# A two-layer diffusion block on one core: fixed gate buffers, a free list of fetch rows, and side work called twice a step

## The chip, the cores and the metric

The kernel runs as one program on one NeuronCore of a Trainium2 chip. The metric is the device time of one execution in microseconds. Three runs of the kernel before took 2971.26, 2975.04 and 2978.68 us; their median, 2975.04 us, is the time before. The core has five instruction streams that run side by side and wait for each other by semaphores: TensorE (PE in the profile; its weight loads are PEld), VectorE (DVE), ScalarE (ACT), GpSimd (POOL) and the stream that issues loads (SP). Each takes its instructions strictly in the order in which they were written.

## The reference

Two layers work on 256 latent tokens and 256 context tokens of width 1024. Each layer mixes tokens (Fourier, pooling and attention branches, gated and projected) and then retrieves experts; the change touches the second half alone:

```python
q = (xc @ wq).reshape(C, PEER_HEADS, 2, PEER_KEY_DIM)
s = jnp.einsum('chpd,hpnd->chpn', q, sub_keys).astype(jnp.float32)
s1, i1 = lax.top_k(s[:, :, 0], PEER_TOPK)
s2, i2 = lax.top_k(s[:, :, 1], PEER_TOPK)
cand = (s1[..., :, None] + s2[..., None, :]).reshape(C, PEER_HEADS, PEER_TOPK * PEER_TOPK)
...
top, pos = lax.top_k(cand, PEER_TOPK)
eidx = jnp.take_along_axis(cidx, pos, axis=-1)
g = jax.nn.softmax(top, axis=-1).astype(xc.dtype)
a = jax.nn.gelu(jnp.einsum('chkd,cd->chk', u_tab[eidx], xc))
return jnp.einsum('chk,chkd->cd', g * a, v_tab[eidx])
```

Each token picks 128 of 16384 experts (8 heads, 16 each). An expert is a row of U and a row of V, 1024 numbers each; a layer's two tables have 64 MB each. The output of layer 1 is that of the latent tokens alone, so layer 0 handles four blocks of 128 tokens and layer 1 two.

## The kernel before, in words

**Dense and fetched blocks.** For all blocks but one the kernel does not gather rows. It multiplies the tokens by the whole table U, applies gelu, multiplies by a gate matrix G (tokens by experts, zero where an expert was not picked) and then by V. In layer 0 three blocks go this way (384 columns) and the fourth is fetched: 128 picks of U rows and 128 of V rows, each a gather of one row per token (`ask`, L945) that VectorE multiplies and sums (`use_one`, L966). In layer 1 both blocks are dense (256 columns) and nothing is fetched.

**The loop over U** (L1114 to L1150) has 64 steps of 256 experts. A step loads 1 MB of U (`raw`, three buffers, L218), transposes it on VectorE (`u_T`, UT, L1011), splits it into a high half on ScalarE (`u_hi`, L1018) and a low half on GpSimd (`u_lo`, L1025), and multiplies: two halves `a` of 24 matmuls each (L282 to L284), each closed by a gelu on ScalarE (L1130). H goes to DRAM (L1132). The transpose runs two steps ahead of the matmuls in layer 0, three in layer 1.

**Side work.** A Python generator, `side`, writes the instructions that pick experts and build G: the top-16 searches on VectorE, then `places` for each block (ending in a reduce of `ii` on VectorE, L854, three transposes on TensorE, L864 to L866, and gL on VectorE, L871), then `gate_matrix`. It yields a cost after each piece. `pump`, called at the end of every step, adds a budget to a debt and goes on writing pieces while the debt is over 2.0; a negative cost means that nothing can be done yet. The budget of a step is 5.4 in layer 0 and 3.2 in layer 1, and 6.6 and 3.8 once the gate matrix has begun. These numbers only set the order in which instructions are written; nothing in the program measures them.

**The gate matrix** takes 8 tokens at a time, a chunk: 48 chunks in layer 0, 32 in layer 1. VectorE writes one-hots by comparing (L890 and L892) and multiplies one of them by the gate (L897; in layer 0 GpSimd does the other half of that multiply, L896; in layer 1 VectorE does it all in L902, and L904 is a part of the low gate); ScalarE scales the one-hots by the low part of the gate (`oh[:, 3]`, L899 or L907). These four one-hots stand in `ohs`, which holds two chunks. TensorE multiplies them, 16 matmuls of 128 columns (L919, L920), and ScalarE moves the two PSUM banks into `stg` (L922). Four chunks fill one `stg`, which ScalarE's queue stores to DRAM as a part of G (L924, 2 MB). In an iteration for chunk c the one-hots of c are written first and the products of c - 1 after them; since `pump` may stop at any yield, the boundary of a call falls in different places. Step 54 writes whatever is left.

**Rows for fetches.** `picked` is two buffers of four rows. Eight rows rotate up to pick 80, four up to pick 128, then eight again, by the fixed table `slot`; a buffer is given back at pick 80 and taken again in the loop over V. In layer 0 112 of the 256 picks are spread over the U loop.

**Buffers.** The pool `b16` has eight buffers of 16 KB a partition for `hl` (split U or V), `hT`, `picked`, `ohs`, `stg`, X and the parts of G and H read back; `b4` has six of 4 KB for gelus, scores and small work. PSUM has six banks for this stage in layer 0, one of them held by `iop`.

**The loop over V** then reads G and H back and multiplies by V, with the same prefetch (`v_load` at step 56 issues the first reads of G on SP's queue).

Of the kernel before, what the change touches and what calls it, by code (L numbers as in the profile page):

```python
# [18 lines left out]
D = 1024  # L19
# [41 lines left out]
def kernel(ctx_: ExitStack, tc: tile.TileContext, I, C, out):  # L61
# [706 lines left out]
    def peer(l, nrm, kT, nb, fin):  # L768
# [52 lines left out]
        def places(b, gT, gL):  # L821
            if True:
# [33 lines left out]
                if b == sparse:  # L856
# [3 lines left out]
                    SP["buf"] = [b16([128, 4, D], name="picked") for _ in range(2)]  # L860
                    SP["ready"] = True
                    return
                ps = psum()
# [10 lines left out]
        def gate_matrix(gT, gL):  # L874
            W = 8
            ohs = b16([128, 2, 4, W, 128], F16, name="ohs")
            hot[0] = True
            iop = psum(name="iop")
            nc.vector.tensor_copy(out=iop[:, :128], in_=iota)
            prev = None  # L880
            stg = None
            for c in range(nt // W + 1):
                cur = None
                if c < nt // W:
                    b, t0 = divmod(c * W, 128)
                    t = gT[b]
                    oh = ohs[:, c % 2]
                    io = iop[:, None, :128].to_broadcast([128, W, 128])
                    bc = lambda q: t[:, q, t0:t0 + W, None].to_broadcast([128, W, 128])
                    nc.vector.tensor_tensor(out=oh[:, 1], in0=io, in1=bc(0), op=OP.is_equal)  # L890
                    yield 1.2
                    nc.vector.tensor_tensor(out=oh[:, 0], in0=io, in1=bc(1), op=OP.is_equal)  # L892
                    if nb == 4:
                        w = W // 2
                        g16 = t[:, 2, t0:t0 + W, None].to_broadcast([128, W, 128])
                        nc.gpsimd.tensor_tensor(out=oh[:, 2, w:], in0=oh[:, 1, w:], in1=g16[:, w:], op=OP.mult)  # L896
                        nc.vector.tensor_tensor(out=oh[:, 2, :w], in0=oh[:, 1, :w], in1=g16[:, :w], op=OP.mult)  # L897
                        for q in range(W):
                            nc.scalar.activation(oh[:, 3, q], oh[:, 1, q], AF.Copy, scale=gL[b][:, t0 + q:t0 + q + 1])  # L899
                        yield 2.2  # L900
                    else:
                        nc.vector.tensor_tensor(out=oh[:, 2], in0=oh[:, 1], in1=bc(2), op=OP.mult)  # L902
                        w = 3
                        nc.vector.tensor_tensor(out=oh[:, 3, :w], in0=oh[:, 1, :w],  # L904
                                                in1=gL[b][:, t0:t0 + w, None].to_broadcast([128, w, 128]), op=OP.mult)
                        for q in range(w, W):
                            nc.scalar.activation(oh[:, 3, q], oh[:, 1, q], AF.Copy, scale=gL[b][:, t0 + q:t0 + q + 1])  # L907
                        yield 2.8
                    cur = (c, oh)
                if prev is not None:  # L910
                    pc, oh = prev
                    if pc % 4 == 0:
                        stg = b16([128, 128, 32], name="stg")
# [12 lines left out]
                prev = cur  # L926


        SP = {"ready": False, "asked": 0, "used": 0}

        DEEP, AGAIN = 80, 128
        slot = [k % 8 if k < DEEP or k >= AGAIN else k % 4 for k in range(256)]
        held = [max((j for j in range(k) if slot[j] == slot[k]), default=-1) for k in range(256)]

        def place(k):
            return SP["buf"][slot[k] // 4][:, slot[k] % 4, :]

        def ask(lag):

            while SP["asked"] < 256 and held[SP["asked"]] < SP["used"] - lag:  # L940
                k = SP["asked"]
                if k >= DEEP and slot[k] > 3 and len(SP["buf"]) == 1:
                    return
# [35 lines left out]
        def picks(upto):  # L979
# [4 lines left out]
            while SP["used"] < min(upto, 256):  # L984
                use_one()
                if SP["used"] == DEEP:
                    SP["buf"].pop()
# [378 lines left out]
```

## Time and profile before

| what | us |
|---|---|
| median of three runs | 2975.04 |
| profiled execution | 2972.67 |
| its span | 2970.7 |
| layer 0, loop over U before the gate matrix | 616 to 804 |
| layer 0, gate matrix | 804 to 1139 |
| layer 0, rest of the loop over U | 1139 to 1317 |
| layer 0, loop over V | 1317 to 1815 |
| layer 1, loop over U before the gate matrix | 2153 to 2296 |
| layer 1, gate matrix | 2296 to 2559 |
| layer 1, rest of the loop over U | 2559 to 2617 |
| layer 1, loop over V and end | 2617 to 2971 |

The span is shared out by stretches that I cut where the first and last instructions of L922 and L1130 stand. In a list of waits, `A x L1 <- B y L2: 21.4, 6, 5.0` means that engine A idled 21.4 us in 6 places, 5.0 at the longest, before it could run line L1 on tile x, and that B's line L2 came last of what it waited for. In a table of stretches an engine's busy time is followed by its number of instructions; the clock is the share of TensorE's full speed that was granted.

### The profile page before, as it was taken

To read this page: it belongs to the slowest core of one execution; us is meant where nothing else is said; L and a number is where in the kernel's file an instruction comes from. 1 tells how busy PE (TensorE), PEld (TensorE's weight loads), DVE (VectorE), ACT (ScalarE), POOL (GpSimd) and SP (SyncE) were. 2 spreads that over 40 slices of the span, in tenths; PEclk is the share of its full clock that TensorE was granted. 3 is DMA by queue.
4 is the path that set the end of the run, shared out by engine and by line. 5 is a ranking of instruction groups with operands and counts; after the bars stand their busy time and mean duration, and the time that the engine had idled before them with its cause. 6 is when DMAs were issued, how large, how long until landed. Compare 5 with 4: busy or idle time off the path is not lost. (4 is left out here: it accounts for less than half of the span.)

```text
span 2970.7 us, 42722 instructions
## 1 busy us (share of the span) xinstructions
PE 2744.0 (92%) x16484; PEld 2410.0 (81%) x16484; DVE 2129.9 (72%) x3388; ACT 1371.9 (46%) x2243; POOL 1277.4 (43%) x698
## 2 busy tenths in 40 slices
PE   6999998798988889999999998999898979899999
PEld 4767796688878889988888886879888979888887
DVE  3444255898979986468999998546797778466666
ACT  3443222233478874333333333544444777544443
POOL 0110002246767767766666663110578666610000
PEclk9999998899999999999999999999999989999999
DMA  6215655558989989999999996426788899988775
GB/s 230 87 43 192 238 183 183 157 136 209 237 234 299 295 236 299 244 305 388 373 384 370 368 384 240 143 78 200 147 189 190 226 219 220 234 284 306 284 288 201
DMA packets 365580, 706.99 MB, mean 238 GB/s; under 512 B 25424, under 2 KB 265456, under 8 KB 351296
## 3 DMA queue, kind: packets, MB, share of 16 engines
q1 hardware_dynamic: 271104, 491.38, 55.4%
q0 software_dynamic: 36864, 134.23, 12.7%
q10 hardware_dynamic: 57408, 78.65, 7.7%
q8 instruction: 129, 2.11, 0.3%
q14 instruction: 75, 0.61, 0.1%
HBM read 619.18 MB, written 85.00 MB: 237 GB/s over the span
## 5 line engine op out<-in xcount | busy, mean ns | idle before, releaser
L1176 PE MATMUL acc<-hl,A 128*128 128x512 f32 x3840 | 870.9, 389 | 0.2 <-ACT A L287 0.2
L1176 PEld LDWEIGHTS acc<-hl,A 128*128 128x128 f32 x3840 | 720.8, 188 | 149.8 <-ACT A L287 0.4
L1025 POOL TENSOR_TENSOR hl<-UT,hl 128x1024 fp32r<-128x1024 f32 x256 | 634.8, 2503 | 375.6 <-ACT hl L1018 363.7
L289 POOL TENSOR_TENSOR hl<-raw,hl 128x1024 fp32r<-128x1024 f32 x112 | 276.7, 2482 | 694.3 <-ACT hl L287 573.8
L287 ACT ACTIVATE hl<-raw 128x1024 fp32r<-128x1024 f32 x388 | 387.7, 1047 | 243.1 <-PE acc L1176 71.4
L289 DVE TENSOR_TENSOR hl<-raw,hl 128x1024 fp32r<-128x1024 f32 x276 | 354.2, 1315 | 123.1 <-ACT hl L287 122.5
L282 PE MATMUL ps<-hTh,hl 128*128 128x384 f32 (+2 forms) x1168 | 411.9, 353 | 6.8 <-ACT hl L1018 6.8
L1011 DVE STREAM_TRANSPOSE UT<-raw 128x2048 f32<-128x2048 f32 x128 | 294.4, 2302 | 171.9 <-DMA raw<-in_peer_u_dram 120.3
L284 PE MATMUL ps<-hTh,hl 128*128 128x384 f32 (+2 forms) x1168 | 408.1, 349 | 7.7 <-POOL hl L1025 6.8
L283 PE MATMUL ps<-hTl,hl 128*128 128x384 f32 (+2 forms) x1168 | 407.1, 349 | 3.5 <-POOL hTl L289 3.5
L284 PE MATMUL ps<-hT,hl 128*128 128x256 f32 x1152 | 332.3, 288 | 9.9 <-POOL hl L1025 9.9
L282 PE MATMUL ps<-hT,hl 128*128 128x256 f32 x1152 | 335.9, 292 | 1.6 <-ACT hl L1018 1.6
L1018 ACT ACTIVATE hl<-UT 128x1024 fp32r<-128x1024 f32 x256 | 256.3, 1050 | 166.3 <-DVE UT L1011 153.8
L283 PE MATMUL ps<-hT,hl 128*128 128x256 f32 x1152 | 331.8, 288 | 0.8 <-POOL hT L289 0.8
L287 ACT ACTIVATE A<-af 128x768 fp32r<-128x768 f32 (+1 forms) x128 | 94.5, 738 | 344.2 <-PE acc L1176 182.2
L282 PEld LDWEIGHTS ps<-hTh,hl 128*128 128x128 f32 x1168 | 229.5, 196 | 19.9 <-ACT hl L1018 7.4
L284 PEld LDWEIGHTS ps<-hTh,hl 128*128 128x128 f32 x1168 | 228.6, 196 | 17.8 <-POOL hl L1025 13.0
L284 PEld LDWEIGHTS ps<-hT,hl 128*128 128x128 f32 x1152 | 226.5, 197 | 12.2 <-POOL hl L1025 12.2
L283 PEld LDWEIGHTS ps<-hTl,hl 128*128 128x128 f32 x1168 | 229.3, 196 | 8.0 <-POOL hTl L289 3.7
L282 PEld LDWEIGHTS ps<-hT,hl 128*128 128x128 f32 x1152 | 227.3, 197 | 2.0 <-ACT hl L1018 2.0
L283 PEld LDWEIGHTS ps<-hT,hl 128*128 128x128 f32 x1152 | 227.0, 197 | 1.3 <-POOL hT L289 1.3
L289 DVE TENSOR_TENSOR A<-af,A 128x768 fp32r<-128x768 f32 (+1 forms) x128 | 139.5, 1090 | 117.3 <-ACT A L287 117.2
(246 smaller groups left out, 4729.8 us busy)
## 6 DMA issues: line engine op xcount, KB each, us to landing
raw<-in_peer_u_dram SPq DMA_DIRECT2D x512, 256.0 KB
raw<-in_peer_v_dram SPq DMA_DIRECT2D x128, 1024.0 KB
raw<-in_ada_w_dram SPq DMA_DIRECT2D x48, 1024.0 KB
G<-stg ACTq DMA_DIRECT2D x20, 2048.0 KB
raw<-in_w_in_dram SPq DMA_DIRECT2D x34, 1024.0 KB
Gq<-G SPq DMA_DIRECT2D x16, 1536.0 KB
H<-Hg ACTq DMA_DIRECT2D x56, 384.0 KB
Hq<-H SPq DMA_DIRECT2D x14, 1536.0 KB
```

Of the source, the lines that this page charges most:

```text
L282: nc.tensor.matmul(ps, lhsT=lh, rhs=rh, start=first, stop=False)
L283: nc.tensor.matmul(ps, lhsT=lh, rhs=rl, start=False, stop=False)
L284: nc.tensor.matmul(ps, lhsT=ll, rhs=rh, start=False, stop=last)
L287: nc.scalar.activation(hi, src, AF.Copy)
L289: eng.tensor_tensor(out=lo, in0=src, in1=hi.bitcast(F32), op=OP.subtract)
L1011: nc.vector.transpose(t, r)
L1018: nc.scalar.activation(t[:, 0, a], v[:, a], AF.Copy)
L1025: nc.gpsimd.tensor_tensor(out=t[:, 1, a], in0=v[:, a], in1=t[:, 0, a].bitcast(F32), op=OP.subtract)
L1176: nc.tensor.matmul(acc[b][n], lhsT=a4[:, lhs, a, t], rhs=rhs[:, o:o + 512], start=f, stop=e)
```

## The change

Five edits go together. `gate_matrix` takes two fixed `stg` tiles at its start and uses them in turn. Its loop now writes the products of chunk c - 1 first and the one-hots of c after them, yields 3.3 (layer 0) or 4.6 (layer 1) once per chunk, and then yields None, at which `pump` returns: one chunk a call at most. `places` yields None too, ahead of its transposes. `pump` is called twice a step, after the first gelu and at the end, each with half the budget. The fetch rows come from a list: four of a `b16` buffer before the gate matrix, three single `b4` rows more from its start to step 54, and a second buffer of four from the second step of the loop over V.

```diff
+                yield None
                 ps = psum()
                 nc.tensor.transpose(ps[:, 0:128], ii[:, 0], ident)
...
+            if sparse is not None:
+                more("single")
+            stgs = [b16([128, 128, 32], name="stg") for _ in range(2)]
...
-                if prev is not None:
-                    pc, oh = prev
+                if c:
+                    pc = c - 1
+                    oh = ohs[:, pc % 2]
                     if pc % 4 == 0:
-                        stg = b16([128, 128, 32], name="stg")
+                        stg = stgs[pc // 4 % 2]
...
+                nc.vector.tensor_tensor(out=oh[:, 1], in0=io, in1=bc(0), op=OP.is_equal)
+                if nb == 4:
+                    w = W // 2
+                    nc.gpsimd.tensor_tensor(out=oh[:, 2, w:], in0=oh[:, 1, w:], in1=bc(2, w), op=OP.mult)
+                    nc.vector.tensor_tensor(out=oh[:, 2, :w], in0=oh[:, 1, :w], in1=bc(2, 0, w), op=OP.mult)
+                    w = 0
...
+                for q in range(w, W):
+                    nc.scalar.activation(oh[:, 3, q], oh[:, 1, q], AF.Copy, scale=low[:, q:q + 1])
+                nc.vector.tensor_tensor(out=oh[:, 0], in0=io, in1=bc(1), op=OP.is_equal)
+                yield 3.3 if nb == 4 else 4.6
+                yield None
...
-            while SP["asked"] < 256 and held[SP["asked"]] < SP["used"] - lag:
+            while SP["asked"] < 256 and len(SP["free"]) > lag:
                 k = SP["asked"]
...
+                SP["row"][k] = SP["free"].pop(0)
...
+        def more(kind):
+            if kind == "big":
+                t = b16([128, 4, D], name="picked")
+                SP["free"] += [(t[:, j, :], kind) for j in range(4)]
+            else:
+                SP["free"] += [(b4([128, D], name="picked"), kind) for _ in range(3)]
+            SP["keep"].add(kind)
...
-                c = next(sd, None)
-                if c is None:
+                c = next(sd, 0.0)
+                if c is None or c == 0.0:
                     return
...
                 nc.scalar.activation(Hg[:, a, :], ps[:, :nt], AF.Gelu_apprx_tanh)
+                if a == 0:
+                    pump(per / 2)
...
-            pump(per + (extra if hot[0] else 0.0))
+            pump(per / 2 + (extra if hot[0] else 0.0))
             if st == NSTEP - 10:
-                while next(sd, None) is not None:
+                SP["keep"].discard("single")
+                SP["free"] = [f for f in SP["free"] if f[1] in SP["keep"]]
+                for _ in sd:
                     pass
...
-                if len(SP["buf"]) == 1 and SP["used"] >= AGAIN - 4:
-                    SP["buf"].append(b16([128, 4, D], name="picked"))
+                if m == 1:
+                    more("big")
```

How the order moves, at three places. The first is ScalarE in the gate matrix of layer 0, before, over a step and the start of the next (numbers are those of buffers; H0 and G0 are layer 0's in DRAM):

```order
L1018 ACTIVATE hl_8640<-UT_8503 128x1024 x2
L1130 ACTIVATE Hg_8643<-ps_8644 128x384
L1130 ACTIVATE Hg_8643<-ps_8670 128x384
L1132 DMA H0_9_3482<-Hg_8643 128x768
L899 ACTIVATE ohs_6248<-ohs_6248,gL_6246 128x128 x8
L922 ACTIVATE stg_8579<-ps_8714 128x4x128
L922 ACTIVATE stg_8579<-ps_8724 128x4x128
L899 ACTIVATE ohs_6248<-ohs_6248,gL_6246 128x128 x8
L922 ACTIVATE stg_8579<-ps_8746 128x4x128
L922 ACTIVATE stg_8579<-ps_8756 128x4x128
L924 DMA G0_3472<-stg_8579 128x16x256
L1018 ACTIVATE hl_8775<-UT_8638 128x1024 x2
```

The same engine after, over a step:

```order
L1018 ACTIVATE hl_7591<-UT_7455 128x1024 x2
L1130 ACTIVATE Hg_7594<-ps_7595 128x384
L899 ACTIVATE stg_6288<-ps_7621 128x4x128
L899 ACTIVATE stg_6288<-ps_7631 128x4x128
L901 DMA G0_3472<-stg_6288 128x16x256
L923 ACTIVATE ohs_6284<-ohs_6284,gL_6041 128x128 x8
L1130 ACTIVATE Hg_7594<-ps_7654 128x384
L1134 DMA H0_7_3480<-Hg_7594 128x768
L899 ACTIVATE stg_6289<-ps_7687 128x4x128
L899 ACTIVATE stg_6289<-ps_7697 128x4x128
L923 ACTIVATE ohs_6284<-ohs_6284,gL_6041 128x128 x8
L1018 ACTIVATE hl_7726<-UT_7589 128x1024 x2
```

Before, both gelus stand together and a call of two chunks follows, here one that begins with one-hots and ends with the products of the same one-hots. After, each gelu is followed by one chunk's evictions and the one-hots of the next; the counts in a step are the same. All 48 chunks stand in 24 such steps.

The second place is VectorE before the gate matrix of layer 0, at the end of `places` for the first dense block, before:

```order
L1011 STREAM_TRANSPOSE UT<-raw 128x2048
L966 SCALAR_TENSOR_TENSOR picked,picks<-picked,hrow 128x1024 x2
L852 TENSOR_TENSOR eq<-eq,ft 128x2048
L854 TENSOR_REDUCE ii<-eq 128x128
L871 SCALAR_TENSOR_TENSOR gL<-ps,gT 128x128
```

and after:

```order
L1011 STREAM_TRANSPOSE UT<-raw 128x2048
L852 TENSOR_TENSOR eq<-eq,ft 128x2048
L968 SCALAR_TENSOR_TENSOR picked,picks<-picked,hrow 128x1024 x2
L854 TENSOR_REDUCE ii<-eq 128x128
L1011 STREAM_TRANSPOSE UT<-raw 128x2048
L872 SCALAR_TENSOR_TENSOR gL<-ps,gT 128x128
```

The transposes on TensorE stand between the last reduce and gL in both; a transpose of U has moved between these two on VectorE, and on TensorE 24 matmuls of the next half step now stand ahead of the three transposes.

The third place is ScalarE at the end of the gate matrix of layer 1, before:

```order
L1132 DMA H1_13_16913<-Hg_22195 128x512
L922 ACTIVATE stg_22060<-ps_22251 128x4x128
L922 ACTIVATE stg_22060<-ps_22261 128x4x128
L922 ACTIVATE stg_22060<-ps_22271 128x4x128
L922 ACTIVATE stg_22060<-ps_22281 128x4x128
L924 DMA G1_16899<-stg_22060 128x16x256
L1018 ACTIVATE hl_22299<-UT_22190 128x1024 x2
```

and after, where step 54 writes what is left:

```order
L899 ACTIVATE stg_19132<-ps_22302 128x4x128
L899 ACTIVATE stg_19132<-ps_22312 128x4x128
L923 ACTIVATE ohs_19130<-ohs_19130,gL_19128 128x128 x5
L899 ACTIVATE stg_19132<-ps_22331 128x4x128
L899 ACTIVATE stg_19132<-ps_22341 128x4x128
L923 ACTIVATE ohs_19130<-ohs_19130,gL_19128 128x128 x5
L899 ACTIVATE stg_19132<-ps_22360 128x4x128
L899 ACTIVATE stg_19132<-ps_22370 128x4x128
L923 ACTIVATE ohs_19130<-ohs_19130,gL_19128 128x128 x5
L899 ACTIVATE stg_19132<-ps_22389 128x4x128
L899 ACTIVATE stg_19132<-ps_22399 128x4x128
L901 DMA G1_16891<-stg_19132 128x16x256
```

Before, the last two chunks' products stand together in step 52, with no one-hots left to write. After, three chunks' one-hots and four chunks' products stand in a row in step 54, and the last store of G two steps later than before.

## Rows read from the trace of the kernel before

**Rows 1.** The page: busy us (share) x instructions of each engine.

```profile
PE 2744.0 (92%) x16484; PEld 2410.0 (81%) x16484; DVE 2129.9 (72%) x3388; ACT 1371.9 (46%) x2243; POOL 1277.4 (43%) x698
```

**Rows 2.** Stretches: length; PE, PEld, DVE, ACT, POOL busy (count); clock; DMA; GB/s.

```profile
616.00:804.00 188.00, 164.22 (x910) 162.45 (x909) 173.45 (x361) 68.39 (x93) 129.75 (x62) 0.94 0.78 198
804.00:1139.00 335.00, 285.18 (x1972) 269.36 (x1971) 292.30 (x273) 273.26 (x581) 227.17 (x150) 0.91 0.93 268
888.00:1009.00 121.00, 108.59 (x782) 103.16 (x783) 116.67 (x110) 110.11 (x234) 92.09 (x61) 0.96 1.03 300
...
1317.00:1815.00 498.00, 498.00 (x2199) 412.46 (x2198) 462.21 (x406) 172.84 (x187) 326.37 (x205) 1.00 0.95 375
...
2153.00:2296.00 143.00, 122.04 (x968) 120.34 (x968) 125.36 (x228) 64.65 (x101) 113.57 (x44) 0.94 0.87 191
2296.00:2559.00 263.00, 232.55 (x2099) 228.96 (x2098) 204.17 (x155) 193.06 (x352) 159.91 (x66) 0.94 0.90 222
```

**Rows 3.** Waits of PE, 616 to 804: us in total, times, longest.

```profile
PE ps L865 <- DVE ii L854: 19.7, 3, 13.9
```

**Rows 4.** Waits of PE, 804 to 1139.

```profile
PE ps L919 <- POOL ohs L896: 21.4, 6, 5.0
PE ps L919 <- ACT Hg L1130: 12.6, 9, 3.1
```

**Rows 5.** Waits of DVE, 616 to 804.

```profile
DVE picked L966 <- DMA picked<-in_peer_u_dram,picks: 5.3, 2, 4.2
DVE gL L871 <- ACT gT L869: 3.7, 3, 1.4
```

**Rows 6.** Stretch 804 to 1139, line 922 alone: ACT busy (count).

```profile
804.00:1139.00 335.00, 97.57 (x96) 0.91 0.93 268
```

**Rows 7.** The same stretch, line 1130 alone.

```profile
804.00:1139.00 335.00, 22.80 (x51) 0.91 0.93 268
```

**Rows 8.** ACT groups, 888 to 1009: busy, mean ns | idle before.

```profile
L899 ACT ACTIVATE ohs<-ohs,gL 128x128 f16<-128x128 f16 x152 | 46.0, 388 | 2.3 <-ACT stg L922 2.3
L922 ACT ACTIVATE stg<-ps 128x512 f32<-128x512 f32 x40 | 41.3, 1141 | 8.3 <-PE ps L920 5.1 <-issue 2.8 <-ACT Hg L1130 0.4
L1018 ACT ACTIVATE hl<-UT 128x1024 fp32r<-128x1024 f32 x20 | 19.9, 1045 | 0.0
L1130 ACT ACTIVATE Hg<-ps 128x384 f32<-128x384 f32 x22 | 9.4, 473 | 0.2 <-PE ps L284 0.2
```

**Rows 9.** ACT in order of time, 905 to 950: start, us.

```profile
912.38 0.33 ACTq L1132 DMA_DIRECT2D H<-Hg  x1
```

**Rows 10.** Stretch of plain steps, columns as in rows 2.

```profile
1139.00:1222.00 83.00, 83.00 (x481) 83.00 (x480) 39.93 (x46) 29.77 (x41) 63.03 (x37) 1.00 0.92 257
```

**Rows 11.** Waits of PE, 2150 to 2620.

```profile
PE ps L919 <- DVE ohs L902: 24.9, 5, 9.2
PE ps L865 <- DVE ii L854: 13.5, 2, 10.0
```

**Rows 12.** Stretches, line 966 alone: DVE busy (count).

```profile
616.00:804.00 188.00, 18.83 (x32) 0.94 0.78 198
1139.00:1317.00 178.00, 48.46 (x83) 0.97 0.95 267
```

**Rows 13.** Waits of DVE, 1139 to 1317.

```profile
DVE picked L966 <- DMA picked<-in_peer_u_dram,picks: 25.9, 13, 4.3
```

**Rows 14.** DVE in order of time, 2295 to 2400.

```profile
2342.38 1.19 DVE L890 TENSOR_TENSOR ohs<-iop,gT 128x1024 f16<-128x1024 f32 x1
...
2346.21 2.30 DVE L1011 STREAM_TRANSPOSE UT<-raw 128x2048 f32<-128x2048 f32 x1
```

**Rows 15.** Waits of DVE, 2550 to 2617.

```profile
DVE UT L1011 <- DMA raw<-in_peer_u_dram: 31.9, 6, 12.6
```

**Rows 16.** Waits of DVE, 2295 to 2550.

```profile
DVE UT L1011 <- DMA raw<-in_peer_u_dram: 53.4, 15, 7.2
```

**Rows 17.** Line 897: ns min/median/max, first and last start.

```profile
L897 DVE TENSOR_TENSOR ohs<-ohs,gT x48: 673/1513/2635, 802.1 to 1123.5; 128x512 f16<-128x512 f16 x48
```

More of the change, by code (lines that the diff above doesn't have):

```diff
@@ L859, in places @@
                     nc.vector.tensor_copy(out=SP["rows"][:, 2, :].bitcast(U32), in_=f)
-                    SP["buf"] = [b16([128, 4, D], name="picked") for _ in range(2)]
+                    more("big")
                     SP["ready"] = True
                     return
+                yield None
                 ps = psum()
@@ L877, in gate_matrix @@
             hot[0] = True
+            if sparse is not None:
+                more("single")
+            stgs = [b16([128, 128, 32], name="stg") for _ in range(2)]
             iop = psum(name="iop")
             nc.vector.tensor_copy(out=iop[:, :128], in_=iota)
-            prev = None
             stg = None
             for c in range(nt // W + 1):
[L883 to L909, printed above, removed]
-                if prev is not None:
-                    pc, oh = prev
@@ L925, in gate_matrix @@
                                             in_=stg.rearrange("p (g i) t -> p g (i t)", g=16))
[L926 to L936, printed above, removed]
+                if c == nt // W:
+                    return
@@ new lines, in gate_matrix @@
+                b, t0 = divmod(c * W, 128)
+                t = gT[b]
+                oh = ohs[:, c % 2]
+                io = iop[:, None, :128].to_broadcast([128, W, 128])
+                bc = lambda q, lo=0, hi=W: t[:, q, t0 + lo:t0 + hi, None].to_broadcast([128, hi - lo, 128])
+                low = gL[b][:, t0:t0 + W]
+                nc.vector.tensor_tensor(out=oh[:, 1], in0=io, in1=bc(0), op=OP.is_equal)
[5 more added lines that the diff above has]
+                else:
+                    w = 3
+                    nc.vector.tensor_tensor(out=oh[:, 2], in0=oh[:, 1], in1=bc(2), op=OP.mult)
+                    nc.vector.tensor_tensor(out=oh[:, 3, :w], in0=oh[:, 1, :w],
+                                            in1=low[:, :w, None].to_broadcast([128, w, 128]), op=OP.mult)
@@ L938, in ask @@
+                for q in range(w, W):
[3 more added lines that the diff above has]
+                yield None
+        SP = {"ready": False, "asked": 0, "used": 0, "row": {}, "free": [], "keep": set()}
         def ask(lag):
-            while SP["asked"] < 256 and held[SP["asked"]] < SP["used"] - lag:
+            while SP["asked"] < 256 and len(SP["free"]) > lag:
@@ L941, in ask @@
                 k = SP["asked"]
-                if k >= DEEP and slot[k] > 3 and len(SP["buf"]) == 1:
-                    return
                 name = "peer_u" if k < 128 else "peer_v"
+                SP["row"][k] = SP["free"].pop(0)
                 nc.gpsimd.indirect_dma_start(
-                    out=place(k), out_offset=None, in_=I[name].rearrange("l e d -> (l e) d"),
+                    out=SP["row"][k][0], out_offset=None, in_=I[name].rearrange("l e d -> (l e) d"),
                     in_offset=bass.IndirectOffsetOnAxis(ap=SP["rows"][:, 2, k % 128:k % 128 + 1].bitcast(U32), axis=0))
@@ L962, in use_one @@
             k = SP["used"]
-            row = place(k)
+            row, kind = SP["row"].pop(k)
+            if kind in SP["keep"]:
+                SP["free"].append((row, kind))
             e, dots = SP["rows"][:, 0, :], SP["rows"][:, 3, :]
@@ L985, in picks @@
                 use_one()
-                if SP["used"] == DEEP:
-                    SP["buf"].pop()
                 if SP["used"] < upto:
@@ L1162, in peer @@
             if sparse is not None:
-                if len(SP["buf"]) == 1 and SP["used"] >= AGAIN - 4:
-                    SP["buf"].append(b16([128, 4, D], name="picked"))
+                if m == 1:
+                    more("big")
                 picks(USTEPS + (256 - USTEPS) * (m + 1) // (NSTEP - 2))
```

1 line of the change is left out of this document (added).

## The prediction

> **What bounds the kernel now.** I read the page first: TensorE is busy 92% of the span [rows 1], so whatever idles it counts. The table by stretches then says where that is [rows 2]. In the loop over V of layer 0 TensorE has no gap (498.00 of 498.00 us): nothing that the change does there can show. The gaps lie in the two loops over U. In layer 0 that loop has a part before the gate matrix (616 to 804 us, TensorE 164.22 of 188), the gate matrix (804 to 1139, 285.18 of 335) and a plain rest; in layer 1 there are the same parts, 2153 to 2296 and 2296 to 2559 the first two.
>
> Next I read whom TensorE waits for. Before the gate matrix of layer 0 it is three waits, 19.7 us, of the transposes of `ii` for VectorE's reduce [rows 3]. In the gate matrix it is the products at L919: 21.4 us for GpSimd's half of a one-hot multiply and 12.6 for ScalarE, which frees their PSUM [rows 4]. Then I looked at whether the engine that is waited for is itself full. Before the gate matrix VectorE is busy 173.45 us [rows 2] and waits 5.3 us for fetched rows and 3.7 for ScalarE [rows 5]: 182.5 of 188 us. It is the bound there, and TensorE's wait is where its backlog shows. In the gate matrix no engine is full: ScalarE 273, TensorE 285 and VectorE 292 of 335.
>
> That stretch is uneven, though. It has 96 evictions, two to a chunk, so 48 chunks [rows 6], and 51 gelus, two to a step, so 25 steps [rows 7]: 13.4 us a step. From 888 to 1009 us there are 40 evictions [rows 8], ten steps of two chunks in 121 us, 12.1 each; the other fifteen take 214 us, 14.3 each. In the even piece both products of a call have their one-hots in the call before; in the rest the second has them in its own call, GpSimd has the low half of U and the fetches to do before its part of them, and TensorE stands behind it. In the even piece ScalarE has least air: 110.11 of 121 us busy, beside the time that its transfers take to issue.
>
> **The change part by part.** *Products one call behind, one chunk a call, two calls a step (layer 0).* Nothing is removed: the same one-hots, evictions and matmuls are issued. What goes is the order that made TensorE wait for one-hots of its own call. What is late next is ScalarE, whose order is an eviction pair, eight one-hots and a gelu, twice a step, and the high half of U. Its step is worked out from the even piece [rows 8]: four evictions at 41.3/40 = 1.03 are 4.13, sixteen one-hots at 46.0/152 = 0.303 are 4.84, two halves of U at 19.9/20 are 1.99, two gelus at 9.4/22 are 0.85, one issue of H and half a one of G at 0.33 [rows 9] are 0.50; together 12.3 us. Beside it VectorE needs 116.67/10 = 11.7, TensorE 108.59/10 = 10.9, GpSimd 92.09/10 = 9.2 [rows 2]: covered, VectorE by little. If that cover is gone the step is VectorE's (a rival below). The built order has two chunks in each of 24 steps, so the 25 steps become 24 at 12.3 and one plain one. A plain step is 83.00 us for 481 matmuls, 48 a step, or 8.3 [rows 10]. 24 x 12.3 + 8.3 = 304, against 335: **-31 us**. If the pace of the whole stretch stayed at 13.4 the gain would be a chunk's worth or nothing (0); if TensorE's 10.9 decided, 24 x 10.9 + 8.3 = 270, or -65. I take ScalarE's sum, since ten steps of the trace run at that pace.
>
> *Two fixed gate buffers.* An eviction may fill the second while the first is being stored. In the even piece ScalarE waits 8.3 us in front of evictions, 5.1 of it for TensorE and 2.8 for its own issue [rows 8], none for the store. I count 0 (-3 to 0); four chunks' work lies between two stores and hides them.
>
> *Transposes a call later.* They stand behind 24 more matmuls on TensorE. That would cover much of the 19.7 us in layer 0 and of 13.5 in layer 1 [rows 11], were VectorE not full; in layer 1 it is busy 125.36 of 143 us [rows 2]. I count 0 for TensorE (-33 to 0). VectorE gets a transpose of U between its reduce and gL, which may take up the 3.7 us that it waits there [rows 5]: -3.
>
> *Fetch rows.* Before the gate matrix four rows rotate instead of eight, so a row asked for in one step is used in the next, and VectorE, the bound there, may wait. It makes 16 picks before 804 us (32 rows, two to a pick [rows 12]). The nearest row is the rest of layer 0, through most of which four rows rotate (from pick 80): 25.9 us waited [rows 13] in front of some 42 picks [rows 12], 0.6 each, so 10 us for 16. VectorE comes later to its picks where it is full, so I take half, +5; the ends are 0 and the whole 26. In the gate matrix seven rows rotate for about two picks a step: nothing, as with eight before. GpSimd issues as many fetches as before, and its first burst, ahead of a low half of U, is four and not eight. In the loop over V eight rows come back some steps earlier, under a full TensorE: nothing.
>
> *A chunk costs 4.6 instead of 4.0 in layer 1.* At 3.8 a step the pace falls from 0.95 to 0.83 chunks a step, and the order leaves three chunks for the flush at step 54. VectorE needs 3.83 us for one (2342.38 to 2346.21 [rows 14]), 11.5 for three. TensorE waits for them; U's loads go on meanwhile, and after 2550 VectorE waited 31.9 us for such loads [rows 15]. Cost: 0 if those cover it; 11.5 + 9.2, the longest wait of TensorE for one-hots there [rows 11], if not. I take +3. The rest of that gate matrix stays as it is: VectorE is busy 204.17 us [rows 2] and waits 53.4 for U [rows 16], 258 of 263, so that TensorE's 24.9 us there [rows 11] are again VectorE's backlog.
>
> Sum: -31 - 3 + 5 + 3 = -26. The profiled execution took 2972.67 us (span 2970.7 and 2.0 around it), so 2946.7; it lies 2.4 below the median of the three runs, 2975.04. Against the median I forecast **2949 us**.
>
> A rule that speaks against this rests on one row: the gate multiply of VectorE, L897, takes 673 ns at least, 1513 in the middle and 2635 at most [rows 17]. The Trainium skill, SBUF — State Buffer, section "Who interferes with whom", says that a VectorE instruction with two inputs in SBUF and a GpSimd instruction that reads SBUF shut each other out for the whole of the one that came first. The trace agrees in that L897 is the one VectorE form here with two such inputs and a fourfold spread. By the rule the price depends only on what GpSimd is doing at that instant, and the new order places VectorE's multiply right behind GpSimd's.
>
> **The rivals.** *Slower: VectorE's multiply always meets GpSimd.* Place: both calls of each step in the gate matrix of layer 0. If each L897 takes its maximum instead of its middle value, VectorE's step is 11.7 + 2 x 1.12 = 13.9 us, over ScalarE's 12.33: 24 x 13.9 + 8.3 = 342, +7, and with +5 in the other terms +12: 2987 against the median. It decides from 13.4 us a step, where the gate matrix gains nothing. For it: VectorE is only 0.6 us below ScalarE, and GpSimd is busy 227 of 335 us. Against it: half of the multiplies meet GpSimd already.
>
> *The end of layer 1 gives it back.* The flush costs its 20.7 us in full, since the last store of G now comes two steps before it is read again: -26 + 18 = -8, so 2967. For it: TensorE waited up to 9.2 us at such a place [rows 11]. Against it: the loads are late there anyway.
>
> *TensorE's waits go as well.* If the delayed transposes do free TensorE, 19.7 + 13.5 more go: 2916. Against it: VectorE is full in both stretches.
>
> **How the numbers follow.** My forecast has 0.55, and 2934 to 2963 is its own range. The transposes' rival has 0.12, the end of layer 1 0.20, the multiply 0.13. The range leaves out the far half of the first and about half of the last: 2914 to 2987. A measurement of this kernel tells 0.3%, 9 us, from no change: faster is below 2966, slower above 2984. Faster: 0.55 + 0.12 + 0.08 of the layer 1 case, 0.75. Slower: 0.10 of the multiply and 0.02 of layer 1, 0.12. The rest is 0.13.
>
> **What would show it.** Right: the gate matrix of layer 0 takes about 304 us, 12.3 a step in every step; L919 waits for GpSimd no more, and the remaining waits name ScalarE's one-hots; the stretch before it stays near 188; in layer 1 one knot of four products near the end and no change before. Wrong: gate steps still alternate; L897 rises above 2 us in the middle; VectorE waits more than 10 us for fetches before the gate matrix; or the loops over V, which I hold untouched, change length.

## The result and the profile after

The changed kernel takes 2943.76 us (median of five runs, 2938.56 to 2944.16) against 2975.04: a ratio of 0.9891, 95% interval 0.9878 to 0.9905. It is faster by 1.1%. I forecast 2949. The profiled execution has a span of 2942.0 us, 28.7 less than before. The sum of the terms came out 3 us off, but three of them by 11 or 12, in both directions, so that the close sum is in part luck; the stretches show it.

The first view is the table by stretches of the kernel after, cut as in [rows 2]:

```profile
616.00:795.00 179.00, 165.34 (x919) 163.65 (x919) 178.09 (x366) 72.12 (x102) 119.72 (x56) 0.95 0.80 201
...
795.00:1103.00 308.00, 290.96 (x1967) 259.60 (x1964) 286.04 (x274) 270.33 (x574) 241.33 (x154) 0.98 1.00 292
...
1275.00:1773.00 498.00, 497.96 (x2197) 411.77 (x2196) 474.28 (x408) 173.11 (x187) 328.40 (x205) 1.00 0.95 375
...
2110.00:2250.00 140.00, 124.59 (x992) 122.31 (x993) 123.80 (x226) 65.19 (x101) 110.74 (x43) 0.96 0.88 194
2250.00:2516.00 266.00, 229.82 (x2008) 227.09 (x2007) 209.55 (x145) 183.07 (x327) 161.35 (x68) 0.93 0.89 215
2516.00:2590.00 74.00, 66.88 (x551) 65.97 (x550) 35.56 (x28) 38.16 (x64) 38.02 (x16) 0.91 0.82 227
```

Read the lengths against [rows 2]. Layer 0: the part before the gate matrix 188 to 179, the gate matrix 335 to 308, the rest 178 to 172. The loop over V has 498 in both. Layer 1: 143 to 140, 263 to 266, and the end of the loop over U from 58 to 74. VectorE is busy 178.09 of the first 179 us.

The waits of TensorE, 616 to 795 and then 795 to 1103 us, answer to [rows 3] and [rows 4]:

```profile
PE ps L866 <- DVE ii L854: 8.3, 2, 4.5
```

```profile
PE ps L897 <- ACT ohs L923: 7.5, 11, 2.6
PE ps L896 <- POOL ohs L914: 5.4, 1, 5.4
```

The wait for the reduce of `ii` has fallen from 19.7 to 8.3 us. In the gate matrix the 21.4 us for GpSimd's half are one wait of 5.4 at the start. What remains names ScalarE's one-hots. The even part of the gate matrix, from its third step on:

```profile
826.00:1084.00 258.00, 247.18 (x1679) 218.31 (x1677) 247.22 (x236) 234.92 (x504) 200.82 (x128) 0.99 0.99 296
```

These are 21 steps (84 evictions), 12.29 us each on average (one takes 15.43), with ScalarE busy 234.92 us beside its issues. TensorE looks nearly full (247.18), but part of that is waiting, as its matmuls show. ScalarE and then TensorE in order of time, in one half step:

```profile
833.62 2.09 ACT L899 ACTIVATE stg<-ps 128x512 f32<-128x512 f32 x2
835.47 2.42 ACT L923 ACTIVATE ohs<-ohs,gL 128x128 f16<-128x128 f16 x8
837.76 0.50 ACT L1130 ACTIVATE Hg<-ps 128x384 f32<-128x384 f32 x1
```

```profile
835.78 0.23 PE L896 MATMUL ps<-ohs 128*128 128x128 f16 x1
835.89 0.22 PE L897 MATMUL ps<-ohs 128*128 128x128 f16 x1
...
836.18 0.22 PE L897 MATMUL ps<-ohs 128*128 128x128 f16 x1
...
836.48 0.22 PE L897 MATMUL ps<-ohs 128*128 128x128 f16 x1
```

Each L897 starts 0.29 or 0.30 us behind the last, the time of one of ScalarE's eight one-hots. TensorE follows ScalarE product by product, which the list of waits shows only in part. So ScalarE does hold TensorE up, as the prediction had it. VectorE, busy 247.22 of the 258 us, is as near to full, and no run parts the two.

The end of layer 1, VectorE in order of time, and TensorE's wait from 2510 to 2590 us:

```profile
2517.52 2.29 DVE L1011 STREAM_TRANSPOSE UT<-raw 128x2048 f32<-128x2048 f32 x1
2519.75 1.18 DVE L911 TENSOR_TENSOR ohs<-iop,gT 128x1024 f16<-128x1024 f32 x1
...
2532.49 1.22 DVE L924 TENSOR_TENSOR ohs<-iop,gT 128x1024 f16<-128x1024 f32 x1
2533.62 2.30 DVE L1011 STREAM_TRANSPOSE UT<-raw 128x2048 f32<-128x2048 f32 x1
```

```profile
PE ps L896 <- DVE ohs L924: 13.3, 4, 6.1
```

Between two transposes of U lie 13.9 us of one-hots for the chunks that step 54 writes, and TensorE waits 13.3 us for them.

### The profile page after: what moved, and what is told of

Read it like the earlier page. It is cut to its first block, busy times and chain, and to the rows that moved or that the text cites. A ratio compares the mean times of both kernels' runs of the same rounds, so it can differ in the third digit from the quotient of the medians.

```text
span 2942.0 us, 42776 instructions
## 1 busy us (share of the span) xinstructions
PE 2753.4 (94%) x16484; PEld 2403.8 (82%) x16484; DVE 2158.2 (73%) x3388; ACT 1375.9 (47%) x2243; POOL 1282.2 (44%) x698
## 3 DMA queue, kind: packets, MB, share of 16 engines
q0 software_dynamic: 36864, 134.23, 12.5%
## 5 line engine op out<-in xcount | busy, mean ns | idle before, releaser
L282 PE MATMUL ps<-hTh,hl 128*128 128x384 f32 (+2 forms) x1168 | 407.9, 349 | 4.2 <-ACT hl L1018 4.2
L284 PE MATMUL ps<-hTh,hl 128*128 128x384 f32 (+2 forms) x1168 | 402.0, 344 | 6.1 <-POOL hl L1025 6.1
L282 PEld LDWEIGHTS ps<-hTh,hl 128*128 128x128 f32 x1168 | 224.8, 192 | 20.9 <-issue 4.9
L284 PEld LDWEIGHTS ps<-hTh,hl 128*128 128x128 f32 x1168 | 224.6, 192 | 12.1 <-POOL hl L1025 7.4
```

The source lines that it names most:

```text
L282: nc.tensor.matmul(ps, lhsT=lh, rhs=rh, start=first, stop=False)
L284: nc.tensor.matmul(ps, lhsT=ll, rhs=rh, start=False, stop=last)
```

## The experiments

Twelve kernels, each timed in five rounds beside the kernel before on the same chip. The last three columns are us between the starts of gelus in the profiled executions: steps 0 to 18 and 19 to 43 of layer 0 (before the gate matrix, and the gate matrix), and 54 to 63 of layer 1. Where the code is the same, the first of these columns repeats within 0.3 us (184.4 in before, even_phase and uneven_phase), but the other two differ by up to 4 (307.7 in after and 311.5 in cost38; 58.9 in before and 62.8 in uneven_phase), so a smaller difference there says nothing.

| kernel | median us | ratio to before, 95% interval | 0-18 | 19-43 | 54-63 |
|---|---|---|---|---|---|
| before | 2975.04 | 1 | 184.4 | 334.6 | 58.9 |
| after | 2943.76 | 0.9891 (0.9878 to 0.9905) | 174.6 | 307.7 | 72.9 |
| even_phase | 2938.46 | 0.9867 (0.9852 to 0.9882) | 184.4 | 296.3 | 61.1 |
| uneven_phase | 3014.98 | 1.0129 (1.0114 to 1.0145) | 184.4 | 376.4 | 62.8 |
| end_calls | 3027.16 | 1.0164 (1.0151 to 1.0177) | 179.8 | 390.3 | 76.5 |
| one_stg | 3037.97 | 1.0192 (1.0173 to 1.0212) | 174.7 | 407.8 | 72.8 |
| cost38 | 2937.02 | 0.9865 (0.9850 to 0.9880) | 174.4 | 311.5 | 59.9 |
| no_stop | 2958.49 | 0.9942 (0.9929 to 0.9956) | 188.0 | 306.2 | 72.7 |
| cost38_four | 2955.66 | 0.9923 (0.9909 to 0.9936) | 174.5 | 320.9 | 60.1 |
| spread_rows | 2934.96 | 0.9870 (0.9849 to 0.9891) | 174.5 | 311.4 | 58.3 |
| even_stop | 2933.77 | 0.9852 (0.9838 to 0.9866) | 183.8 | 300.1 | 57.6 |
| even_stop_burst | 2935.65 | 0.9874 (0.9854 to 0.9893) | 178.7 | 310.1 | 57.6 |
| even_stop_spread | 2948.53 | 0.9908 (0.9883 to 0.9933) | 179.0 | 317.2 | 57.6 |
| psum_operand | 2922.22 | 0.9809 (0.9789 to 0.9830) | 171.5 | 299.4 | 57.6 |

### Is it the phase of the calls?

Before, two chunks cost 2 x (1.2 + 2.2) = 6.8 and a step gives 6.6, so the place in a chunk at which a call stops drifts, and only ten of 25 steps are even. Two kernels hold it still, in the good place and in the bad one; nothing else of the change is in them.

```diff
             hot[0] = True
+            if nb == 4:
+                debt[0] = 0.4      # uneven_phase: 5.8
...
-        per, extra = (5.4, 1.2) if nb == 4 else (3.2, 0.6)
+        per, extra = (5.4, 1.4) if nb == 4 else (3.2, 0.6)
```

even_phase:

> The kernel before with two numbers changed, in layer 0 alone: the budget of a step in the gate matrix is 6.8, exactly two of its chunks, and the debt is set to 0.4 at its start, so that in every step both products stand in the call after their one-hots. No half-step calls, no fixed gate buffers, no list of rows. Theory A (the uneven steps came from products in the call of their own one-hots): all 24 steps run at the pace of the even piece, 12.1 us, the gate matrix takes 335 - 27 = about 308 us and the kernel about 2948, ratio 0.991. Theory B (the half-step calls or the second gate buffer did it): steps stay at 13.4 on average, ratio 0.998 to 1.002.

uneven_phase:

> The same as the run before it, but with the debt set to 5.8, so that in every step the second product stands in the call of its own one-hots. Theory A: all 24 steps run at the pace of the uneven steps of the trace, 14.3 us, 24 x 14.3 + 8.3 = 352 us instead of 335, about 2992 us, ratio 1.006. Theory B: as in the other phase, ratio 0.998 to 1.002.

Two numbers alone, with 48 chunks, one-hots and products unchanged, give 2938.46 or 3014.98. Both go the way of theory A and beyond its size (2948 and 2992). TensorE's waits in the gate matrix (805 to 1101 us), first even, then uneven:

```profile
PE ps L921 <- ACT Hg L1132: 24.6, 18, 2.6
```

```profile
PE ps L921 <- POOL ohs L898: 49.7, 12, 6.2
```

In the uneven kernel every second step takes about 18.6 us and the others 12.05; in this window TensorE waits for GpSimd's half multiply 12 times, 4.1 us on average. The even one has 25 steps in 296.3 us, fewer than the changed kernel. So the whole gain in the gate matrix can be had from the phase.

end_calls: the changed kernel, with both calls at the end of the step.

```diff
                 nc.scalar.activation(Hg[:, a, :], ps[:, :nt], AF.Gelu_apprx_tanh)
-                if a == 0:
-                    pump(per / 2)
...
+            pump(per / 2)
             pump(per / 2 + (extra if hot[0] else 0.0))
```

> The changed kernel with both calls at the end of the step, none after its first gelu. Products are still one chunk behind their one-hots and a call still has one chunk at most; but the second chunk's products come right behind the one-hots of the first in the same place of the step. Theory A: what counts is the work that lies between one-hots and their products, and here there is none in front of every second product, so the gate matrix of layer 0 goes back to an alternating pace, 350 to 376 us instead of 308, and the kernel to 2985 to 3010 us, slower than before; the waits name GpSimd's half multiply or ScalarE's one-hots. Rival: one chunk behind is enough, wherever the call stands, and the time stays within 8 us of 2944.

Right in sign and beyond the expected size. The waits of TensorE and of VectorE, 800 to 1190 us:

```profile
PE ps L897 <- ACT ohs L923: 52.6, 22, 2.8
```

```profile
DVE ohs L915 <- PE ps L896: 92.4, 21, 5.3
```

Nearly once a step TensorE stands some 2.4 us for ScalarE's one-hots of the chunk whose products come next, as theory A expected. VectorE's multiply, which overwrites one-hots whose products stand just ahead of it, now waits for TensorE; that alone does not make a step long, for in even_phase it overwrites as closely and waits 0.9 us for TensorE in the whole gate matrix (805 to 1101 us). One chunk behind is not enough; what counts is the work, here 24 matmuls, that lies between the two calls.

### The two gate buffers

```diff
-            stgs = [b16([128, 128, 32], name="stg") for _ in range(2)]
+            stgs = [b16([128, 128, 32], name="stg")] * 2
```

> The changed kernel with one gate buffer in place of two. The prediction's term: 0 to +3 us, 2944 to 2947, since four chunks' work lies between two stores. Rival: the first eviction after a store waits for the store to land (some us each, 12 stores in layer 0 and 8 in layer 1), and with calls at the half step TensorE stands behind it: +10 us or more.

By the ratios some 90 us slower than after, all of it in the gate matrix of layer 0 (100 us by the profiles). ScalarE's waits, 800 to 1210 us, and the two ends of one of them:

```profile
ACT stg L899 <- DMA G<-stg: 116.2, 11, 14.2
```

```profile
921.92 0.38 ACTq L901 DMA_DIRECT2D G<-stg  x1
...
936.17 1.88 ACT L899 ACTIVATE stg<-ps 128x512 f32<-128x512 f32 x2 [11.01 <-DMA G<-stg]
```

From the issue of a store to the eviction that it holds up are 14.25 us, and that eviction stands half a step behind it. ScalarE's queue then holds the one-hots and TensorE. With two buffers four chunks, 24.6 us, lie in between; that cover, which the prediction named, is real and hides some 90 us. In layer 1 the same wait is 9.8 us and costs nothing that shows.

### The stop ahead of the transposes

no_stop: the changed kernel without `yield None` in `places`.

> The changed kernel without the stop ahead of the transposes in places: these stand again in the call of their reduce. Theory A (the delayed transposes gave the 9 us before the gate matrix of layer 0): TensorE waits some 15 to 20 us for the reduces there again, the stretch goes back from 179 to 186 to 188, layer 1 by 3, and the kernel to about 2955, ratio 0.993. Theory B (the smaller first burst of fetches gave it, VectorE being full): within 3 us of the changed kernel, ratio 0.988 to 0.990.

Theory A held: the stretch before the gate matrix goes back to 188.0 us and the kernel loses 0.5% against after. Waits of TensorE there, 616 to 808 us:

```profile
PE ps L865 <- DVE ii L854: 22.5, 3, 8.7
```

even_stop: the kernel before with the even phase and the stop, and nothing else that moves the order (the loop that writes what is left at step 54 now runs on past a stop).

```diff
+                yield None
                 ps = psum()
                 nc.tensor.transpose(ps[:, 0:128], ii[:, 0], ident)
```

> The kernel before with two edits: the even phase of the calls in layer 0 (as in even_phase, where it alone gave 2938.5 us), and the transposes of places written one call, here a whole step, later. There are no calls at the half step, no second gate buffer, no row list. Theory A: the stop is worth what no_stop took away, some 13 us in the stretch before the gate matrix of layer 0 (184 to about 173) and 4 in layer 1, and it is independent of the calls at the half step; so about 2922 us, ratio about 0.981, below the changed kernel, and the waits of L865 for the reduce of ii are gone from that stretch. Rival: the stop helps only together with the calls at the half step (or VectorE is full there, as the prediction had it), and the time is within 4 us of even_phase, 2935 to 2942.

The wait for `ii` fell as expected, but the stretch kept its length. TensorE's waits, 616 to 805 us, and VectorE and GpSimd in order of time:

```profile
PE ps L284 <- POOL hl L1028: 12.5, 4, 8.0
PE ps L866 <- DVE ii L854: 4.3, 2, 3.7
```

```profile
729.18 9.73 DVE L852 TENSOR_TENSOR eq<-eq,ft 128x2048 f16<-128x2048 f16 x1
```

```profile
717.28 1.09 POOL L948 DMA_INDIRECT picked<-in_peer_u_dram,picks  x1 [0.17 <-POOL hl L1028]
...
728.47 9.34 POOL L1028 TENSOR_TENSOR hl<-UT,hl 128x1024 fp32r<-128x1024 f32 x4
```

GpSimd issues eight fetches from 717.28 on, then does four low halves in a row, to 737.81. VectorE's L852, a multiply of two operands in SBUF that takes 1.20 us at its shortest, starts at 729.18 and ends at 738.91, 1.10 us behind GpSimd.

even_stop_burst shortens that first burst.

```diff
-        slot = [k % 8 if k < DEEP or k >= AGAIN else k % 4 for k in range(256)]
+        slot = [k % 8 if 16 <= k < DEEP or k >= AGAIN else k % 4 for k in range(256)]
```

> The kernel of even_stop (2933.8 us) with one more edit: the first 16 fetched rows rotate through four places and not eight, so that GpSimd's first burst of fetches is four and not eight; from then on eight rotate as before. In even_stop the delayed transposes took TensorE's wait for the reduce of ii from 19.6 to 4.3 us before the gate matrix of layer 0, but the stretch stayed at 184 us: GpSimd issued eight fetches ahead of a low half of U, TensorE waited 12.5 us for that half, and one L852 on VectorE took 9.73 us beside it. Theory A: the stop is worth its 10 us only where the burst is short, as it is in the changed kernel; the stretch falls to about 174, the kernel to about 2924 us, ratio 0.982. Rival: the stop needs the calls at the half step, and the time stays at 2930 to 2937.

Half of it: 178.7 us instead of 183.8 there, but 10 us more in the gate matrix, most of it in step 20 (17.66 us), where I take it that the other four rows come at once. In total no change that can be told. L852 met GpSimd again, VectorE and then GpSimd:

```profile
728.28 4.68 DVE L852 TENSOR_TENSOR eq<-eq,ft 128x2048 f16<-128x2048 f16 x1
```

```profile
722.48 9.38 POOL L1028 TENSOR_TENSOR hl<-UT,hl 128x1024 fp32r<-128x1024 f32 x4
```

It ends at 732.96, again 1.10 us behind GpSimd's end at 731.86. So I took away what would make VectorE stand aside: psum_operand is even_stop with the second operand of L848 and L852 in PSUM, in layer 0.

```diff
+                cmp = iota
+                if nb == 4:
+                    cmp = psum(name="pq")
+                    nc.vector.tensor_copy(out=cmp[:, :16], in_=iota[:, :16])
-                tif = ft[:, 1].rearrange("p (h a k) -> p h a k", h=8, a=2)
+                tif = (cmp[:, 256:512] if nb == 4 else ft[:, 1]).rearrange("p (h a k) -> p h a k", h=8, a=2)
...
-                                            in1=iota[:, None, :16].to_broadcast([128, 128, 16]), op=OP.is_equal)
+                                            in1=cmp[:, None, :16].to_broadcast([128, 128, 16]), op=OP.is_equal)
```

> The kernel of even_stop (ratio 0.9852), where in layer 0 the second operand of the compare and of the multiply of places (the iota, and the picks' high halves) lies in PSUM and not in SBUF; one bank is held for it. In even_stop these two lines take 54.5 us of VectorE before the gate matrix (8 times 3.34 and 8 times 3.48; at their shortest, 2.25 and 1.17, they would take 27), and the longest, 9.73 us, ended 1.10 us behind the last of four low halves on GpSimd. Theory A: VectorE is shut out there while GpSimd reads SBUF, and only with two operands in SBUF; so the spread goes, each line takes 2.2 to 2.4 us every time (the second may lose its fast form of 1.17), together about 37 us, the stretch before the gate matrix falls from 184 to about 172 and the ratio to about 0.981. Rival one: the spread has another cause and stays, and the time with it (0.984 to 0.987). Rival two: the spread goes, but TensorE waits for the low half of U behind eight fetches as before (8.0 us at step 12), and the stretch stays at 180 or more, the ratio within 0.002 of even_stop's.

Theory A held in every number. VectorE's two lines before the gate matrix, in even_stop as groups (616 to 810 us; busy, mean ns), in psum_operand one by one (616 to 796 us; ns min/median/max):

```profile
L852 DVE TENSOR_TENSOR eq<-eq,ft 128x2048 f16<-128x2048 f16 x8 | 27.8, 3481 | 0.2
L848 DVE TENSOR_TENSOR eq<-ft,iota 128x2048 f16<-128x2048 f16 x8 | 26.7, 3343 | 0.0
```

```profile
L856 DVE TENSOR_TENSOR eq<-eq,pq x8: 2247/2286/2290, 686.0 to 784.5; 128x2048 f16<-128x2048 f16 x8
L852 DVE TENSOR_TENSOR eq<-ft,pq x8: 2272/2276/2281, 683.7 to 782.2; 128x2048 f16<-128x2048 f16 x8
```

54.5 us became 36.5 (8 x 2.286 + 8 x 2.276), although the multiply lost its short form; each of the 16 now takes 2.25 to 2.29 us. The stretch fell by 12.3 us and the kernel to 2922.22, below both kernels of the case and all others here.

### The fetched rows and the end of layer 1

cost38: the changed kernel with a chunk at 3.8 in layer 1, so that nothing is left for step 54.

```diff
-                yield 3.3 if nb == 4 else 4.6
+                yield 3.3 if nb == 4 else 3.8
```

> The changed kernel with a chunk cost of 3.8 instead of 4.6 in layer 1, the budget of a step, so that each step of the gate matrix writes one chunk and none is left at step 54. Theory A (the three chunks left for step 54 cost the 14 us by which the last ten steps of layer 1 grew): that stretch falls from 73 to about 59 us and the kernel is 12 to 15 us faster than the changed one, about 2930, ratio 0.985. Theory B (the end of layer 1 is late because of its last store of G or the loads behind it, wherever the chunks stand): no more than 4 us faster, ratio 0.988 to 0.990.

The last ten steps went from 72.9 to 59.9 us, as theory A said. The kernel gained less, 0.26% or 8 us. In the two profiles the gate matrix of layer 0, whose code is the same, is 3.8 us longer, and the first 21 steps of layer 1 are 5.8 us longer, of which the last already holds a chunk that the cheaper cost moved; I can't tell more.

cost38_four: cost38 without the three single rows (`more("single")` left out).

> The changed kernel with a chunk at cost 3.8 in layer 1 (as in cost38, 2937.0 us) and without the three single fetch rows: four rows rotate through the whole loop over U of layer 0. Theory A: the three extra fetches that GpSimd issues at the start of the gate matrix, ahead of its half of the multiply, cost 5 to 7 us there, and four rows are enough for about two picks a step; so about 2931 us, and steps 18 and 19 are near 14 us instead of 16.6 and 18.9. Rival: with four rows VectorE waits for fetched rows in the gate matrix and in the rest of layer 0 (0.6 us a pick, some 60 picks there), and the time is 2945 to 2970.

The rival held: it is 0.6% slower. VectorE's wait for rows in the gate matrix (797 to 1118 us), which is 0.6 us in cost38:

```profile
DVE picked L966 <- DMA picked<-in_peer_u_dram,picks: 45.9, 23, 10.6
```

spread_rows: cost38 with the three rows handed out one at a time, at chunks 1, 3 and 5.

> The changed kernel with a chunk at cost 3.8 in layer 1 (cost38, 2937.0 us), and the three single fetch rows handed out one at a time, with the second, fourth and sixth chunk of the gate matrix, not all three at its start. Theory A: the burst of five fetches ahead of GpSimd's half multiply makes steps 18 and 19 long (16.6 and 18.9 us); spread out it is gone, both steps are near 14, the gate matrix of layer 0 falls from 311 to about 304 and the kernel to about 2930 us. Rival: what is long there is the first chunks' one-hots on a VectorE that is still behind, and the time stays at 2934 to 2940.

Step 19 fell from 18.9 to 12.5 us, as theory A said, but step 18 only from 16.6 to 15.1, and others rose: step 20 from 12.2 to 14.0 and step 33 from 12.1 to 16.9. The gate matrix has 311.4 against 311.5 in cost38. The rival's time held; its reason was not tried.

even_stop_spread: even_stop_burst with its second four rows added at picks 24, 32, 40 and 48.

> The kernel of even_stop_burst (2935.7 us), with the second four fetched rows added one at a time, at picks 24, 32, 40 and 48, in place of all four in one call. There the stretch before the gate matrix fell from 184 to 179 us, and the gate matrix rose from 300 to 310, with one step of 17.66 us (5.5 MB in it) where the second four rows were asked for. Theory A: that step is the second burst, and it goes: 179 before the gate matrix and 300 to 302 in it, so about 2927 us, ratio about 0.983, the lowest of all here. Rival: the rise is not the burst's (the stretches of one profile differ by some 4 us between kernels with the same code), and the time stays at 2932 to 2937.

Neither: it is slower than even_stop (against even_stop_burst the intervals meet), its gate matrix grew once more, to 317.2 us, and its runs spread from 2939.89 to 2961.76. So the rise in even_stop_burst is not shown to be the second burst's. Why is open.

## Why the prediction came out right

Differences of the stretches of the two profiles beside the terms.

| term | forecast | measured |
|---|---|---|
| gate matrix of layer 0 | -31 | -27 |
| transposes (and gL) | -3 | -10 in layer 0, -4 in layer 1 (near the noise) |
| fetch rows | +5 | no wait before the gate matrix; rest of layer 0 -7 |
| end of layer 1 | +3 | +14 |
| loops over V | 0 | 0 |
| sum (with +4 in layer 1's gate matrix, +1 elsewhere) | -26 | -29 |

The gate matrix alone gives the forecast its size. The other terms, +5 together, came out at -2, but only because the misses cancel: that is luck.

**The gate matrix** was right in mechanism and nearly in size: 12.29 us a step where I had 12.3 for ScalarE (the terms add to 12.31; the 12.33 under the rivals is a slip on which nothing hangs), and no alternation of long and short steps in 21. What the sum did not have are the first two steps, 16.60 and 18.88 us. There GpSimd issues five fetches (three for the single rows) ahead of its half multiply, but spread_rows, which hands those rows out singly, has as long a gate matrix, so that their price isn't shown:

```profile
799.08 1.26 POOL L937 DMA_INDIRECT picked<-in_peer_u_dram,picks  x1
...
804.37 1.19 POOL L937 DMA_INDIRECT picked<-in_peer_u_dram,picks  x1 [0.30 <-issue]
805.58 2.04 POOL L914 TENSOR_TENSOR ohs<-ohs,gT 128x512 f16<-128x512 f16 x2
```

What I didn't see is that before was a matter of phase alone: I read ten even steps and fifteen uneven ones without asking what set the count, though 6.6 against 6.8 stood in the code. even_phase shows that the step of the prediction "in the even piece both products of a call have their one-hots in the call before" was the whole answer there.

**The transposes** are the step that failed: "I count 0 for TensorE", because VectorE was full. VectorE was busy 173.45 of 188 us [rows 2]; the prediction added 9.0 us of its waits [rows 5] to that and called the 182.5 the bound. Waits are not load, and two more stood beside them, 616 to 804 us:

```profile
DVE gsum L841 <- ACT picks L830: 3.1, 1, 3.1
DVE gsum L841 <- ACT ge L830: 1.7, 3, 1.1
```

In the kernel after VectorE's idle time has gone from 14.6 to 0.9 us (178.09 busy of 179), and TensorE's wait for the reduce from 19.7 to 8.3. no_stop brings both back, 9.8 us of VectorE's waits (8.1 of them for fetched rows) and 22.5 of TensorE's, so the stop is worth 13 us there. The calls at the half step have a part in it: end_calls, which has all else of the change, takes 179.8 us instead of 174.6, and VectorE waits 7.5 us there (616 to 799 us). Why the rows come in time with the stop and late without it is open.

VectorE's busy time is not all work either. L848 and L852 stand aside for GpSimd, before and then after, 616 to 810 us:

```profile
L848 DVE TENSOR_TENSOR eq<-ft,iota 128x2048 f16<-128x2048 f16 x8 | 20.3, 2543 | 0.0
L852 DVE TENSOR_TENSOR eq<-eq,ft 128x2048 f16<-128x2048 f16 x8 | 16.6, 2081 | 0.2
```

```profile
L848 DVE TENSOR_TENSOR eq<-ft,iota 128x2048 f16<-128x2048 f16 x8 | 25.9, 3234 | 0.0
L852 DVE TENSOR_TENSOR eq<-eq,ft 128x2048 f16<-128x2048 f16 x8 | 13.6, 1704 | 0.1
```

That is 36.9 and 39.5 us, where 16 at their shortest in the kernel after would take 27 (8 x 2.25 + 8 x 1.17): the change gained nothing from these lines. In even_stop they grew to 54.5 us, and the stop by itself was worth less than 1 us; in psum_operand they take 36.5 and the stretch falls to 171.5. No run has the PSUM operand without the stop, so what each is worth apart is open.

**The fetch rows** had the wrong sign. VectorE never waited for a row before the gate matrix (I had 5, at most 26), and in the rest of layer 0 its wait fell from 25.9 us [rows 13] to 13.1, since seven rows rotate up to step 54 where four did before from pick 80. cost38_four bears this out: with four rows the time from the last gelu of step 43 to that of step 63 is 176.0 us, in cost38 170.3. I had costed the smaller number of rows and not the larger one.

**The end of layer 1** is a term that I undersized: 13.9 us of VectorE, 13.3 us of TensorE's wait and +14 in all, nearer to the 11.5 + 9.2 of its upper end than to 3. "U's loads go on meanwhile" was no cover: VectorE's wait for them did fall, from 31.9 us [rows 15] to 7.2 (2516 to 2590 us), but VectorE is what transposes U, so a load that lands early is still late.

**The rivals.** The slower one, VectorE's multiply always meeting GpSimd, fell: its median went down, against [rows 17]:

```profile
L915 DVE TENSOR_TENSOR ohs<-ohs,gT x48: 691/694/2855, 792.7 to 1081.7; 128x512 f16<-128x512 f16 x48
```

Its mechanism was real, and stood elsewhere: I took L897 for the one line with that spread and passed over L848 and L852, which carry it before the gate matrix. The Trainium skill, SBUF — State Buffer, section "Who interferes with whom", says that a VectorE instruction with two SBUF inputs and a GpSimd one that reads SBUF shut each other out, the later one for the whole of the earlier, and that one with at most one SBUF input, outside the modes that use both of VectorE's port pairs, is free of it. The traces agree on who is shut out: L852 waited out GpSimd and ended 1.10 us behind it twice, and the picks, whose second input lies in PSUM, kept 1180 to 1224 ns in all 128 in the kernel after. By the rule as I used it the price was on the gate multiply, whose median fell in the new order.

## What to carry to other kernels

Where a list of instructions is cut by a budget, compare the budget of a call with the cost of a whole number of pieces: a remainder makes the cut drift, and here its place decided between 0.987 and 1.013. Put other work of the same queue, here 24 matmuls, between a producer's call and its consumer's. An engine that looks full is not thereby the bound: don't add its waits to its load, and compare the shortest and the mean time of each of its lines; where they differ, ask which engine it meets.

## What the runs showed of the hardware that I had not expected

In even_stop VectorE was shut out not for one GpSimd instruction but for a run of them: 8.63 us, from 729.18 to 737.81, across the rest of four in a row. One operand moved to PSUM took all of that away in psum_operand, even where it doubled the line's shortest time (1.17 to 2.25 us).

Where TensorE waited more its granted clock was lower, as a mean over the two levels, 1.2 and 2.4 GHz: in the gate matrix of layer 0 it was 0.97 and 0.98 in even_phase and after, 0.91 before [rows 2], and 0.86 in one_stg:

```profile
797.00:1205.00 408.00, 304.57 (x1968) 277.15 (x1966) 300.44 (x274) 268.29 (x574) 241.99 (x154) 0.86 0.77 220
```

```profile
805.00:1101.00 296.00, 269.76 (x1968) 257.38 (x1967) 291.76 (x271) 273.50 (x580) 218.25 (x148) 0.97 1.00 295
```

What that adds to the waits themselves was not measured apart.
